# Rotary embedding on one core: who asks for the first rows, and what the first load waits for

## The chip, the core and the metric

The kernel runs on one core of one Trainium2 chip. The metric is the device time of one execution in microseconds (us). The profile describes one execution; its span is the part of it that the trace covers.

## The reference

The input x has 8 batches, 2048 positions, 16 heads and 64 values a head, all float32. Each head's vector is cut into two halves of 32, and the halves are rotated by the cosine and sine of the position:

```python
out1 = x1 * cos - x2 * sin
out2 = x1 * sin + x2 * cos
return np.concatenate([out1, out2], axis=-1)
```

`cos` and `sin` have one row of 32 values for each position. 67.1 MB are read and 67.1 MB are written.

## The kernel before

The 2048 positions are laid over 128 partitions, 16 consecutive positions (called rows here, index j) on each; one batch is a tile of 128 x 16384 elements, held as float16. `buf` has five slots for such tiles, and batch b lies in slot b % 5. The DMA casts float32 to float16 on the way in and back on the way out.

`load`, `store` and `queue` (L57) issue these casting transfers from GpSimd (POOL). `queue` ties each to the one before it, so that all of them stand in one queue in the order that the program writes. This text calls it the ring: the rest of batch 0 (rows 2 to 15), the store of batch 0's row 0, loads of batches 1 and 2 and of 3 and 4, the store of batch 0's other rows, and so on to the store of batch 7's rows 0 to 13. An instruction at the head of POOL's stream that waits for another engine holds up all behind it.

`rotate` is three VectorE instructions on a tile: a product of the swapped halves with signed sine into `v` (L87), a product in place with cosine (L91), and the sum (L93).

Three transfers go by the hardware queues instead: sine by SyncE (SP, L50), cosine by ScalarE (ACT, L51), and `head`, the first two rows of batch 0 on each partition, uncast, by ScalarE (L52). `head` uses the space of slot 4. ScalarE casts sine (L101, and negated in L102) and cosine (L103) to float16 and then the two head rows one after the other (L96). Row 0 is rotated and stored ahead of the rest of batch 0. The loads of batches 3 and 4 need slot 4, and so wait until the head has been cast.

At the end the last two rows of batch 7 are cast to float32 by ScalarE (L127) and stored by SP (L128), after the store of batch 7's rows 0 to 8 has landed.

Of the kernel before, what the change touches and what calls it, by code (L numbers as in the profile page):

```python
# [1 line left out]

# [4 lines left out]


@with_exitstack  # L10
def kernel(
    ctx: ExitStack,
    tc: tile.TileContext,
    x: bass.AP,
    cos: bass.AP,
    sin: bass.AP,
    out: bass.AP,
):
    nc = tc.nc
    f16 = mybir.dt.float16  # L20
    f32 = mybir.dt.float32

    B, S, H, D = x.shape
    Dh = D // 2
    P = nc.NUM_PARTITIONS
    J = S // P
    SLOTS = 5
    JA = 2
    JE = 2
    JF = 1  # L30

    pool = ctx.enter_context(tc.tile_pool(name="rope", bufs=1))
    buf = pool.tile([P, SLOTS, J, H, D], f16)
    v = pool.tile([P, J, H, D], f16)
    sin_f = pool.tile([P, J, Dh], f32)
    cos_f = pool.tile([P, J, Dh], f32)
    cos_h = pool.tile([P, J, Dh], f16)
    sin_h = pool.tile([P, J, D], f16)

    def words(slot, rows):  # L40
        flat = buf[:, slot, 0 : 2 * rows].rearrange("p j h d -> p (j h d)")
        return flat.bitcast(f32)

    head = words(SLOTS - 1, JA)
    tail = words(SLOTS - 2, JE)
    rows_in = x.rearrange("b (p j) h d -> p b (j h d)", j=J)
    rows_out = out.rearrange("b (p j) h d -> p b (j h d)", j=J)
    W = H * D

    nc.sync.dma_start(out=sin_f, in_=sin.rearrange("(p j) d -> p j d", j=J))  # L50
    nc.scalar.dma_start(out=cos_f, in_=cos.rearrange("(p j) d -> p j d", j=J))  # L51
    nc.scalar.dma_start(out=head, in_=rows_in[:, 0, 0 : JA * W])  # L52

    ring = []

    def queue(dst, src):
        dma = nc.gpsimd.dma_start(out=dst, in_=src)  # L57
        if ring:
            tc.add_manual_dep(
                dma.ins,  # L60
                ring[-1].ins.name,
                mybir.DependencyInfo(mybir.DependencyClass.NoSync, mybir.DependencyReason.DATA),
                reason="order of the ring",
            )
        ring.append(dma)
        return dma

    def part(b, n, j0, j1):
        s = b % SLOTS
        return buf[:, s : s + n, j0:j1].rearrange("p n j h d -> p n (j h d)")  # L70

    def load(b, n=1, j0=0):
        return queue(part(b, n, j0, J), rows_in[:, b : b + n, j0 * W : J * W])

    def store(b, n=1, j0=0, j1=J):
        return queue(rows_out[:, b : b + n, j0 * W : j1 * W], part(b, n, j0, j1))

    def rotate(b, j0=0, j1=J):
        n = j1 - j0
        js = slice(j0, j1)  # L80
        xt = buf[:, b % SLOTS, js]
        vt = v[:, js]
        shape = [P, n, H, 2, Dh]
        sin_b = sin_h[:, js, :].rearrange("p j (e d) -> p j e d", e=2).unsqueeze(2).to_broadcast(shape)
        cos_b = cos_h[:, js, :].unsqueeze(2).to_broadcast([P, n, 2 * H, Dh])
        xe = xt.rearrange("p j h (e d) -> p j h e d", e=2)
        nc.vector.tensor_mul(  # L87
            out=vt.rearrange("p j h (e d) -> p j h e d", e=2), in0=xe[:, :, :, ::-1, :], in1=sin_b
        )
        xw = xt.rearrange("p j h (e d) -> p j (h e) d", d=Dh)  # L90
        nc.vector.tensor_mul(out=xw, in0=xw, in1=cos_b)  # L91
        xa = xt.rearrange("p j h d -> p (j h d)")
        nc.vector.tensor_add(out=xa, in0=xa, in1=vt.rearrange("p j h d -> p (j h d)"))  # L93

    def narrow_head(j0, j1):
        nc.scalar.copy(  # L96
            out=buf[:, 0, j0:j1].rearrange("p j h d -> p (j h d)"), in_=head[:, j0 * W : j1 * W]
        )

    load(0, j0=JA)  # L100
    nc.scalar.copy(out=sin_h[:, :, Dh:D], in_=sin_f)  # L101
    nc.scalar.mul(out=sin_h[:, :, 0:Dh], in_=sin_f, mul=-1.0)  # L102
    nc.scalar.copy(out=cos_h, in_=cos_f)  # L103
    narrow_head(0, JF)
    narrow_head(JF, JA)
    rotate(0, 0, JF)
    store(0, j1=JF)
    load(1, 2)
    load(3, 2)
    rotate(0, JF, J)  # L110
    store(0, j0=JF)
    rotate(1)
    rotate(2)
    store(1, 2)
    load(5)
    load(6, 2)
    rotate(3)
    rotate(4)
    store(3, 2)
    rotate(5)  # L120
    rotate(6)
    store(5, 2)
    rotate(7)
    gate = store(7, j1=9)
    store(7, j0=9, j1=J - JE)

    nc.scalar.copy(out=tail, in_=buf[:, (B - 1) % SLOTS, J - JE : J].rearrange("p j h d -> p (j h d)"))  # L127
    end = nc.sync.dma_start(out=rows_out[:, B - 1, (J - JE) * W : J * W], in_=tail)  # L128
    tc.add_manual_dep(
        end.ins,  # L130
        gate.ins.name,
        mybir.DependencyInfo(mybir.DependencyClass.Sync, mybir.DependencyReason.DATA),
        reason="the last rows go out behind this part",
    )


# [1 line left out]
_INS = ['x', 'cos', 'sin']  # L138
_OUTS = [((8, 2048, 16, 64), 'float32')]


# [23 lines left out]
```

## Time and profile before

| what | value |
|---|---|
| median of 3 runs | 316.4 us (316.4 to 316.58) |
| profiled execution | 316.32 us |
| its span | 314.6 us |
| VectorE busy | 209.1 us, 66% of the span |
| ScalarE busy, GpSimd busy | 6.8 us, 7.9 us |
| software queue (ring) | 99.09 MB by its count, 98.1% of the 16 engines' span |
| SP's and ScalarE's hardware queues | 1.31 MB each, 1.2% and 1.0% |

The queue counts bytes by its packets' sizes, which for a casting transfer differ between the two ends; memory's own count is 67.63 MB read and 67.11 MB written. Lines such as L57 refer to the kernel before. "ACTq" and "SPq" are the parts of ScalarE and SyncE that issue transfers. A time line's row has the start, the duration, the engine, the line, the operation and, in brackets, how long the engine had been idle and what ended that.

### The profile page before, as it was taken

To read this page: it belongs to the slowest core of one execution; us is meant where nothing else is said; L and a number is where in the kernel's file an instruction comes from. 1 tells how busy PE (TensorE), PEld (TensorE's weight loads), DVE (VectorE), ACT (ScalarE), POOL (GpSimd) and SP (SyncE) were. 2 spreads that over 40 slices of the span, in tenths; PEclk is the share of its full clock that TensorE was granted. 3 is DMA by queue.
4 is the path that set the end of the run, shared out by engine and by line. 5 is a ranking of instruction groups with operands and counts; after the bars stand their busy time and mean duration, and the time that the engine had idled before them with its cause. 6 is when DMAs were issued, how large, how long until landed. Compare 5 with 4: busy or idle time off the path is not lost.

```text
span 314.6 us, 113 instructions
## 1 busy us (share of the span) xinstructions
DVE 209.1 (66%) x27; ACT 6.8 (2%) x7; POOL 7.9 (3%) x16
## 2 busy tenths in 40 slices
DVE  0109991089999999999994399903999999200000
ACT  3200000000000000000000000000000000200000
POOL 1020000000000000000000000000000000100000
DMA  7989999999999899999999999999999999999998
GB/s 230 261 193 249 267 200 200 200 267 200 200 200 325 375 500 400 400 400 533 400 200 221 246 200 200 250 217 333 400 517 417 400 400 525 408 400 400 433 425 342
DMA packets 3072, 101.71 MB, mean 323 GB/s; under 512 B 256, under 2 KB 256, under 8 KB 640
## 3 DMA queue, kind: packets, MB, share of 16 engines
q0 software_dynamic: 2496, 99.09, 98.1%
q1 hardware_dynamic: 288, 1.31, 1.2%
q10 hardware_dynamic: 288, 1.31, 1.0%
HBM read 67.63 MB, written 67.11 MB: 428 GB/s over the span
## 4 chain that ended last, share of the span: by engine, by line
DVE 59%; DMA 19%; another core or an unknown queue 7%; ACT 1%; issue 0%; POOL 0%; ACTq 0%; DVEq 0%
DVE v L87 20%; DVE buf L91 20%; DVE buf L93 20%; DMA buf<-in_x_dram 19%; ACT buf L127 1%; ACT buf L96 0%; POOL out_dram L57 0%; ACTq L51 0%; DVEq L87 0%
## 5 line engine op out<-in xcount | busy, mean ns | idle before, releaser
L87 DVE TENSOR_TENSOR v<-buf,sin_h 128x16384 f16<-128x16384 f16 (+2 forms) x9 | 69.7, 7744 | 59.7 <-DMA buf<-in_x_dram 45.3
L91 DVE TENSOR_TENSOR buf<-buf,cos_h 128x16384 f16<-128x16384 f16 (+2 forms) x9 | 69.7, 7744 | 0.3
L93 DVE TENSOR_TENSOR buf<-buf,v 128x16384 f16<-128x16384 f16 (+2 forms) x9 | 69.7, 7744 | 0.3
L57 POOL DMA_DIRECT2D out_dram<-buf x7 | 4.3, 620 | 219.7 <-DVE buf L93 219.7
L127 ACT CAST buf<-buf 128x2048 f32<-128x2048 f16 x1 | 1.9, 1897 | 254.2 <-DVE buf L93 254.2
L57 POOL DMA_DIRECT2D buf<-in_x_dram x5 | 3.4, 679 | 43.0 <-DMA out_dram<-buf 42.2
L96 ACT CAST buf<-buf 128x1024 f16<-128x1024 f32 x2 | 2.0, 1042 | 7.2 <-DMA buf<-in_x_dram 7.2
L101 ACT ACT_TABLE_LOAD x1 | 1.3, 1283 | 1.7 <-PEq L149 1.7
L101 ACT CAST sin_h<-sin_f 128x512 f16<-128x512 f32 x1 | 0.6, 617 | 1.5 <-DMA sin_f<-in_sin_dram 1.5
L102 ACT ACTIVATE sin_h<-sin_f 128x512 f16<-128x512 f32 x1 | 0.6, 624 | 0.0
L103 ACT CAST cos_h<-cos_f 128x512 f16<-128x512 f32 x1 | 0.6, 601 | 0.0
L149 POOL MEMSET const-float32-0.0<- 128x1 f32 x1 | 0.1, 99 | 0.2 <-issue 0.2
L149 POOL MEMSET const-bfloat16-1.0<- 128x1 bf16 x1 | 0.1, 102 | 0.0
L149 POOL MEMSET const-float32-1.0<- 128x1 f32 x1 | 0.1, 99 | 0.0
L149 POOL MEMSET const-uint8-127<- 128x1 uint8 x1 | 0.1, 99 | 0.0
## 6 DMA issues: line engine op xcount, KB each, us to landing
buf<-in_x_dram POOLq DMA_DIRECT2D x3, 8192.0 KB, 57.1
out_dram<-buf POOLq DMA_DIRECT2D x1, 7680.0 KB, 71.7
out_dram<-buf POOLq DMA_DIRECT2D x1, 4608.0 KB, 35.5
buf<-in_x_dram POOLq DMA_DIRECT2D x1, 4096.0 KB, 57.3
buf<-in_x_dram POOLq DMA_DIRECT2D x1, 3584.0 KB, 22.6
out_dram<-buf POOLq DMA_DIRECT2D x1, 2560.0 KB, 41.0
buf<-in_x_dram ACTq DMA_DIRECT2D x1, 1024.0 KB, 12.1
out_dram<-buf SPq DMA_DIRECT2D x1, 1024.0 KB, 8.4
```

What stands on the lines that cost most here:

```text
L57: dma = nc.gpsimd.dma_start(out=dst, in_=src)
L87: nc.vector.tensor_mul(out=vt.rearrange("p j h (e d) -> p j h e d", e=2), in0=xe[:, :, :, ::-1, :], in1=sin_b)
L91: nc.vector.tensor_mul(out=xw, in0=xw, in1=cos_b)
L93: nc.vector.tensor_add(out=xa, in0=xa, in1=vt.rearrange("p j h d -> p (j h d)"))
L96: nc.scalar.copy(out=buf[:, 0, j0:j1].rearrange("p j h d -> p (j h d)"), in_=head[:, j0 * W : j1 * W])
L101: nc.scalar.copy(out=sin_h[:, :, Dh:D], in_=sin_f)
L102: nc.scalar.mul(out=sin_h[:, :, 0:Dh], in_=sin_f, mul=-1.0)
L103: nc.scalar.copy(out=cos_h, in_=cos_f)
L127: nc.scalar.copy(out=tail, in_=buf[:, (B - 1) % SLOTS, J - JE : J].rearrange("p j h d -> p (j h d)"))
L149: nc = _bacc.Bacc("TRN2", target_bir_lowering=False, num_devices=1)
```

## The change

SyncE now asks for sine and then for the head. A new tile `word` of two float32 values on each partition is made; VectorE writes a zero into the first, and ScalarE copies it to the second. Two waits on this copy are added: that of ScalarE's request for cosine, and that of the first software load (the rest of batch 0). Nothing else in the program is changed. ScalarE's first instruction that needs an activation table is now this copy, and the table load stands ahead of it.

```diff
     nc.sync.dma_start(out=sin_f, in_=sin.rearrange("(p j) d -> p j d", j=J))
-    nc.scalar.dma_start(out=cos_f, in_=cos.rearrange("(p j) d -> p j d", j=J))
-    nc.scalar.dma_start(out=head, in_=rows_in[:, 0, 0 : JA * W])
+    nc.sync.dma_start(out=head, in_=rows_in[:, 0, 0 : JA * W])
+    word = pool.tile([P, 2], f32)
+    nc.vector.memset(word[:, 0:1], 0.0)
+    warm = nc.scalar.copy(out=word[:, 1:2], in_=word[:, 0:1])
+    cosine = nc.scalar.dma_start(out=cos_f, in_=cos.rearrange("(p j) d -> p j d", j=J))
+    tc.add_manual_dep(
+        cosine.ins,
+        warm.ins.name,
+        mybir.DependencyInfo(mybir.DependencyClass.Sync, mybir.DependencyReason.DATA),
+        reason="the first rows are asked for ahead of cosine",
+    )
...
-    load(0, j0=JA)
+    tc.add_manual_dep(
+        load(0, j0=JA).ins,
+        warm.ins.name,
+        mybir.DependencyInfo(mybir.DependencyClass.Sync, mybir.DependencyReason.DATA),
+        reason="cosine goes ahead of the ring",
+    )
```

## The prediction

> **What bounds the kernel now.** I read the page first, then the waits, then the time line of the first 30 us, then windows over the whole span, and last the trace's records of single DMA packets (start and duration of each), which no printed view lists; where I use those I say so. The page and the waits of the trace:
>
> ```profile
> DVE 209.1 (66%) x27; ACT 6.8 (2%) x7; POOL 7.9 (3%) x16
> q0 software_dynamic: 2496, 99.09, 98.1%
> HBM read 67.63 MB, written 67.11 MB: 428 GB/s over the span
> ...
> POOL out_dram L57 <- DVE buf L93: 219.7, 6, 74.0
> DVE v L87 <- DMA buf<-in_x_dram: 45.3, 4, 15.3
> POOL buf L57 <- DMA out_dram<-buf: 42.2, 2, 38.2
> ```
>
> VectorE is busy two thirds of the span and waits 45.3 us for loads; the software queue that POOL fills is busy 98.1% of it. So the bound is the software queue, called the ring below. The chain that ended last shows 59% VectorE, which misleads: VectorE's next tile is already waiting in the ring while it works. The windows show it:
>
> ```profile
> 30.00:120.00 90.00, 74.41 (x10) 0.00 (x0) 1.26 (x2) 1.00 1.01 265
> 120.00:300.00 180.00, 126.54 (x15) 1.90 (x1) 3.82 (x6) 1.00 1.01 362
> ```
>
> The last-but-one column, the DMA share, is 1.01 in both: the engines move data all the time. The packet records agree: from 2.6 us (second sine packet) to 313.4 us (end of the last row's packets) each engine has a packet in hand. The 134.74 MB read and written, over those 310.8 us, are 433.5 GB/s, and one load packet alone (57,344 bytes read, next one 2.111 us later, on 16 engines) is 434.6 GB/s. No gap is left in the middle to be won. What can change is the stretch before about 6 us:
>
> ```profile
> 0.73 0.39 ACTq L51 DMA_DIRECT2D cos_f<-in_cos_dram  x1
> 0.74 0.38 SPq L50 DMA_DIRECT2D sin_f<-in_sin_dram  x1
> 1.15 0.47 ACTq L52 DMA_DIRECT2D buf<-in_x_dram  x1
> 1.25 0.67 POOL L57 DMA_DIRECT2D buf<-in_x_dram  x1 [0.80 <-PEq L160]
> 1.65 1.28 ACT L101 ACT_TABLE_LOAD   x1 [1.65 <-PEq L149]
> 4.45 0.62 ACT L101 CAST sin_h<-sin_f 128x512 f16<-128x512 f32 x1 [1.52 <-DMA sin_f<-in_sin_dram]
> 5.51 0.60 ACT L103 CAST cos_h<-cos_f 128x512 f16<-128x512 f32 x1
> 13.26 1.99 ACT L96 CAST buf<-buf 128x1024 f16<-128x1024 f32 x2 [7.15 <-DMA buf<-in_x_dram]
> 16.79 0.53 POOL L57 DMA_DIRECT2D out_dram<-buf  x1 [14.88 <-DVE buf L93]
> 17.31 1.43 POOL L57 DMA_DIRECT2D buf<-in_x_dram  x2
> 23.94 8.16 DVE L87 TENSOR_TENSOR v<-buf,sin_h 128x15360 f16<-128x15360 f16 x1 [7.46 <-DMA buf<-in_x_dram]
> ```
>
> Columns: start, duration, engine, line and operation. The packet records put these requests on the engines so: sine from 1.83, cosine mixed in from 2.69, head packets (0.306 us apart, eight on each engine) from 3.95, first ring packet at 5.78 behind six head packets, then ring and head by turns until the head lands at 13.24. The first ring packet is on the engines 4.5 us after POOL began the request at 1.25.
>
> **The change, part by part.**
>
> Head on SP's queue. It leaves ScalarE's queue (a 0.47 us request) for SP's, behind sine's (0.74 to 1.12), so it is asked for at about 1.15 as before. SP has nothing else until its wait for the last rows at 305.26. Cost 0; what hides it is that cosine's 256 KB no longer stand ahead of it.
>
> Memset of the word on VectorE. POOL's 128x1 memsets take 0.10; the shortest VectorE row, 128x1024, takes 0.69; so 0.10 to 0.69, and VectorE starts at about 0.7. I take 0.10, the same shape. Either way it is over by 1.4, under ScalarE's table load. VectorE's next work is at 14.34 before, about 7.9 after.
>
> The table load moves from L101 to the new copy, from 1.65 to about 0.73 (where ScalarE's first request stands), and ends at 2.01. The copy: 128x1024 takes 1.042 and 128x512 0.617, so 0.83 ns an element and 0.19 us that no element explains; one element takes about 0.19 (at most the 0.60 of the shortest row). It ends at about 2.22.
>
> Cosine's request waits for it: 2.25 at the earliest (0.03 between instructions of one engine), 2.5 if the wait costs what POOL's waits for VectorE cost (L93 ends at 16.48, POOL starts at 16.79). Behind it on ScalarE stand the sine and cosine casts and both head casts. Cosine's packets came 1.95 after its request, so now at 4.2 to 4.5; landing came 3.9 after, so about 6.3 instead of 4.6. VectorE waits for that and then for the casts.
>
> The first load waits too, and everything that POOL issues stands behind it. Copy's end 2.22 plus 0.30 is 2.52 instead of 1.25: 1.27 later. This is the one cost that can reach the end, since the ring never pauses afterwards.
>
> What is won at the front: the head, no longer mixed with 57 KB packets, lands near 6.4 instead of 13.24. Casts of cosine (0.60), of the first head row (1.05), three VectorE products (3 x 0.72) and 0.30 put POOL's store near 10.5 instead of 16.79, and the next loads near 11. None of that shortens the ring: its first load still holds the engines until about 23.4, and the trace has the store's packets at 23.36 directly behind it, although they were asked for at 16.79. The store was early by 6.6 us and will be by 13; that is worth 0. Were that cover gone, each us late would cost one.
>
> So the sum is the ring's delay less the short work that fills it. Short work (sine, head, cosine) is the same as before: it would have ended at 5.78 plus two head packets, 6.40. It stays gapless if head packets follow sine's at about 3.2 (their request ends at 1.62; cosine's packets came 1.95 after theirs began, hence 3.1) and cosine comes before the head is done, near 5.7 (4.2 to 4.5: yes). Against it stands the ring: when were its first packets ready before (R)? At the earliest at 1.92, the end of the request. At the latest about 5.0: a cold first packet of sine takes 0.80 against 0.08 later, and the ring's first packet at 5.78 shows no such bubble, so it was in work 0.8 before. The nearest row on how far ahead an engine takes its packets is at the end: SP asks for the last rows at 305.26, packets of such a request appear 1.1 to 1.95 later, but these come at 310.63, behind five ring packets of 0.755 that were taken before them. If six head packets were likewise taken ahead, R is 5.78 less 6 x 0.306 = 3.94. With 1.27 added and 0.78 for the cold first packet, ring data begins at 3.94 + 2.05 = 5.99, before 6.40: no idle time. With R at 5.0 it is 7.05: 0.65 idle. Below nothing I exclude, since the engines cannot begin before sine's first packet at 1.83, which does not move. I take 0.2, nearer the lower end, by the row at the end of the kernel.
>
> A rule bears on R. The Trainium skill (DMA: Bandwidth & Descriptors, Latency and other measured facts) gives a software request about 1 us to its first byte; as an estimate from that page R would be 2.3 before and 3.5 after, the idle time 0 and the time unchanged. The trace shows 4.5 us to the first packet behind a busy queue, which neither confirms nor refutes it.
>
> Sum: the profiled execution took 316.32 (span 314.6 and 1.7 outside it); with 0.2 it is 316.5. The median of the runs is 316.4, 0.08 above the profiled one, so 316.6.
>
> **The rivals.**
>
> (a) Forecast: the short work covers the ring's delay, 0 to 0.6 idle, 316.4 to 317.0. For it: the ring packets that the last rows waited behind. Chance 0.60.
>
> (b) Slower: ScalarE is not ready for the copy when the table load ends. In the trace the next ScalarE instruction came 1.52 us after that load (2.93 to 4.45), put down to sine; that it could have come sooner is not shown. If ScalarE needs most of that time, the copy ends at about 3.7 and POOL's first load begins at 4.0, 2.77 late: ring data from 3.94 + 2.77 + 0.78 = 7.49 to 8.55, and the engines idle 1.1 to 2.15: 317.5 to 318.6. It decides once the first load is 2.31 late with R at 3.94 (3.94 + 2.31 + 0.78 is 6.40 plus 0.63 idle), so with the copy's end at 3.26; with R at 5.0 it decides at once. Against it: the sine's landing at 0.74 + 3.7 = 4.44 explains the wait fully. Chance 0.20. The Trainium skill has a rule of this kind (ScalarE: Activation LUTs, What ACT_TABLE_LOAD costs): 1283 ns for the load, with which the 1.28 here agrees, and about 1380 ns of drain, which no row here shows.
>
> (c) Slower by less: no such pause, but R was late (5.0) and POOL's wait longer than 0.30: idle 0.65 to 1.0, 317.05 to 317.4. Chance 0.13.
>
> (d) Faster: the earlier store and loads close a hole in the ring near 18 to 24 us. The window from 18 to 24 has a DMA share of 0.86 against 0.97 from 300 to 306; read as idle time that is 0.11 x 6 = 0.66 us, 315.7. Against it: the packet records have no gap there, and the low share comes from how long packets that cross a window's edge are counted. Chance 0.07.
>
> (e) That the change does not do what it says is excluded by the order of the built program: ScalarE's stream is table load, copy, cosine; POOL's first load waits for ScalarE; SP's has sine, head.
>
> **How the numbers follow.** A difference of 0.2% (0.63 us) is about what a measurement of this kernel can tell from no change. (a) is same (0.60); (b) and (c) slower (0.33); (d) faster (0.07). The point is that of (a), 316.6. The range begins at 316.1 (0.3 under the median, for run to run and for a different stagger of the 16 engines, 0.25 us apart at the start), takes in (c) and the lower half of (b), and ends at 318.0, which leaves out (d) and half of (b): under 2 in 10.
>
> **What would show it.** Right: the copy ends near 2.2, POOL's first load begins near 2.5, the head lands near 6.4, POOL's store is asked for near 10.5, and yet VectorE's L87 of the first tile's rest (23.94 before) begins at 24.0 to 24.5, with all later work late by the same. Wrong: first load at 3.5 or later and L87 near 25 or beyond (b); or L87 before 23.9 and SP's last request before 305.2 (d). If L87 is not late but the end is, the cause lies behind the first load and my accounting of one gapless stream falls.

## The result, and the profile after

The changed kernel takes 321.58 us (median of 6 runs, 318.31 to 322.22) against 316.46 us before (316.3 to 316.61). The ratio is 1.0149, with a 95% interval of 1.0123 to 1.0174: slower by 5.1 us, where 316.6 was forecast and 318.0 was the end of the range. One of the six runs took 318.31 and was not profiled; the other five took 321.5 to 322.2. The profiled execution took 321.77 us, its span 320.0 us, 5.4 more than before.

The time line of the changed kernel (start, duration, engine, line, operation; L54 and L55 are the copy and cosine's request, L66 is the ring, L96 VectorE's first product), and from the page the landing times of three requests:

```profile
0.74 1.28 ACT L54 ACT_TABLE_LOAD   x1 [0.74 <-PEq L163]
2.04 0.19 ACT L54 COPY word<-word 128x1 f32<-128x1 f32 x1
2.26 0.36 ACTq L55 DMA_DIRECT2D cos_f<-in_cos_dram  x1
2.53 0.67 POOL L66 DMA_DIRECT2D buf<-in_x_dram  x1 [2.08 <-ACT word L54]
21.72 0.62 ACT L117 CAST cos_h<-cos_f 128x512 f16<-128x512 f32 x1 [17.24 <-DMA cos_f<-in_cos_dram]
22.25 1.99 ACT L105 CAST buf<-buf 128x1024 f16<-128x1024 f32 x2
25.77 0.53 POOL L66 DMA_DIRECT2D out_dram<-buf  x1 [22.57 <-DVE buf L102]
26.30 1.43 POOL L66 DMA_DIRECT2D buf<-in_x_dram  x2
68.17 8.69 DVE L96 TENSOR_TENSOR v<-buf,sin_h 128x16384 f16<-128x16384 f16 x1 [18.25 <-DMA buf<-in_x_dram]
```

```profile
buf<-in_x_dram SPq DMA_DIRECT2D x1, 1024.0 KB, 4.8
...
cos_f<-in_cos_dram ACTq DMA_DIRECT2D x1, 256.0 KB, 19.4
```

Copy, cosine's request and first load stand where the prediction put them (2.03, 2.25, 2.52), and the head lands 4.8 after its request, at about 6. But cosine lands 19.4 us after its request instead of 3.9. ScalarE takes its work in order, so both head casts wait for cosine's cast, and with them the rotation of row 0 and POOL's store, at 25.77 instead of 16.79. Behind that store stand the next loads.

The windows of the changed kernel around that time (last two columns: DMA share, GB/s), and its ring on the page:

```profile
18.00:23.00 5.00, 0.00 (x0) 1.28 (x2) 0.00 (x0) 1.00 0.86 184
23.00:27.00 4.00, 3.61 (x4) 1.23 (x2) 1.23 (x2) 1.00 0.04 14
27.00:31.00 4.00, 4.00 (x1) 0.00 (x0) 0.73 (x2) 1.00 1.11 256
...
q0 software_dynamic: 2496, 99.09, 97.0%
HBM read 67.63 MB, written 67.11 MB: 421 GB/s over the span
```

From 23 to 27 us the engines move next to nothing: the first load is done and the ring is empty. The kernel before has no such window:

```profile
20.00:25.00 5.00, 1.06 (x1) 0.00 (x0) 0.00 (x0) 1.00 1.23 301
25.00:30.00 5.00, 5.00 (x1) 0.00 (x0) 0.00 (x0) 1.00 0.97 210
```

A window can count a packet whole that reaches into the next (from 19 to 20 us the kernel before has a share of 2.13, from 20 to 21 one of 0.00), so the hole is measured from packets. A second loss is not seen in such windows. The completion records of the ring's transfers (mean over the 16 engines, us) show both:

```
                       before    after    difference
first load              23.40    23.25    -0.15
store of row 0          24.63    28.22    +3.59
load of batches 1, 2    63.28    67.62    +4.34
load of batches 3, 4   101.90   107.32    +5.41
store of batch 0's rest 119.99   125.41    +5.41
last part of the ring  310.72   316.13    +5.41
```

The hole is 3.75 us (28.22 less 23.25, less the store's own 1.22). Behind it the two loads take 39.40 and 39.70 us instead of 38.65 and 38.63, together 1.8 more. After 107 us nothing is added. Packet and completion times in this text, as in the prediction, count from a zero about 0.07 us earlier than that of the time lines.

The packet records show how cosine got there. Its packets begin on all engines at 5.25 to 5.46, directly behind the head; the ring's first packets come at 5.72 to 6.42. On 11 engines all eight cosine packets were through by then (completions by 6.41). On five they were not, and from there one 2 KB packet of cosine went for each 57 KB packet of the ring, about 2.2 us a turn: completions at 14.92, 15.03, 19.08, 19.57 and 21.41. A transfer has landed when its last engine has.

**Theory 1**: that mixing, the late store behind it and the hole make the loss. **Theory 2** (rival): the ring's later start makes it. The 1.8 us of slow loads got theories of their own later.

### The profile page after: what moved, and what is told of

Its sections match the earlier page's. It is cut to its first block, busy times and chain, and to the rows that moved or that the text cites. A ratio compares the mean times of both kernels' runs of the same rounds, so it can differ in the third digit from the quotient of the medians.

```text
span 320.0 us, 115 instructions
## 1 busy us (share of the span) xinstructions
DVE 209.1 (65%) x28; ACT 7.0 (2%) x8; POOL 7.9 (2%) x16
## 4 chain that ended last, share of the span: by engine, by line
DVE 58%; DMA 19%; another core or an unknown queue 7%; ACT 2%; issue 0%; POOL 0%; DVEq 0%
DVE v L96 19%; DVE buf L100 19%; DVE buf L102 19%; DMA buf<-in_x_dram 13%; DMA cos_f<-in_cos_dram 6%; ACT buf L141 1%; ACT L54 0%; ACT buf L105 0%; ACT cos_h L117 0%; POOL out_dram L66 0%; ACT word L54 0%; DVEq L96 0%
## 5 line engine op out<-in xcount | busy, mean ns | idle before, releaser
L96 DVE TENSOR_TENSOR v<-buf,sin_h 128x16384 f16<-128x16384 f16 (+2 forms) x9 | 69.7, 7744 | 64.4 <-DMA buf<-in_x_dram 41.8
L66 POOL DMA_DIRECT2D out_dram<-buf x7 | 4.3, 620 | 223.2 <-DVE buf L102 223.2
L66 POOL DMA_DIRECT2D buf<-in_x_dram x5 | 3.4, 679 | 44.9 <-DMA out_dram<-buf 42.8
L54 ACT COPY word<-word 128x1 f32<-128x1 f32 x1 | 0.2, 192 | 0.0
```

Source lines behind the costliest of these rows:

```text
L54: warm = nc.scalar.copy(out=word[:, 1:2], in_=word[:, 0:1])
L96: nc.vector.tensor_mul(out=vt.rearrange("p j h (e d) -> p j h e d", e=2), in0=xe[:, :, :, ::-1, :], in1=sin_b)
```

## The experiments

Each ratio is to the kernel before, measured beside it, with its 95% interval.

**Cosine asked for at once, the load still waiting.**

```diff
+    nc.scalar.dma_start(out=cos_f, in_=...)     # ahead of sine's request, no wait
     nc.sync.dma_start(out=sin_f, in_=...)
     nc.sync.dma_start(out=head, in_=...)
...
-    cosine = nc.scalar.dma_start(out=cos_f, in_=...)
-    tc.add_manual_dep(cosine.ins, warm.ins.name, ...)
```

> The changed kernel, but cosine is asked for by ScalarE at once, ahead of the table load and of the copy; the first software load still waits for the copy (it will start near 2.9, as the request now stands ahead of the copy). Theory 1 (cosine's late request lets its packets take turns with the ring's 2.1 us packets on some engines; it lands at 21.7, the head casts stand behind it on ScalarE, POOL's store of row 0 comes at 25.8 and the ring runs dry from 23.1 to 27.0): cosine lands near 5, the store is asked for before 12, no hole, 316.4 to 317.0. Theory 2 (what costs is the ring's own later start, 2.53 instead of 1.25): the load is as late or later, so 321 or more.

Measured: 316.47 us, ratio 1.0002 (0.9994 to 1.0011). Its time line:

```profile
2.95 0.67 POOL L60 DMA_DIRECT2D buf<-in_x_dram  x1 [2.51 <-ACT word L55]
5.29 0.60 ACT L111 CAST cos_h<-cos_f 128x512 f16<-128x512 f32 x1
10.49 0.53 POOL L60 DMA_DIRECT2D out_dram<-buf  x1 [6.87 <-DVE buf L96]
```

The first load begins 1.7 later than before (1.25), later still than in the changed kernel, and that costs nothing. Cosine's wait is the part that costs. Theory 2 falls.

**The load free, cosine still waiting.** Only the wait of `load(0, j0=JA)` is taken out of the changed kernel.

> The changed kernel, but the first software load does not wait (starts at 1.25 as in the kernel before); cosine still waits for the copy. Theory 1: the ring is there before cosine, cosine takes turns with it on all 16 engines (eight packets of each engine, 2.2 us a turn, from about 5), lands between 20 and 24, the store comes between 24 and 28, hole of 2 to 5 us, 319 to 323. Theory 2 (the ring's late start costs): 316.4.

Measured: 323.98 us, 1.0239 (1.0226 to 1.0252), worse than the whole change and a little beyond what was expected. All 16 engines now mix: cosine's completions lie between 22.9 and 23.9. The time line, and the window in which the ring is empty:

```profile
24.37 0.62 ACT L112 CAST cos_h<-cos_f 128x512 f16<-128x512 f32 x1 [19.68 <-DMA cos_f<-in_cos_dram]
28.43 0.53 POOL L66 DMA_DIRECT2D out_dram<-buf  x1 [26.52 <-DVE buf L102]
...
23.00:27.00 4.00, 1.00 (x2) 2.51 (x3) 0.00 (x0) 1.00 0.02 5
```

The hole is 6.45 us, and the wait on the load, which the prediction counted as the only cost, is what kept 11 engines of the changed kernel clear of the ring.

**The load still later.** In the changed kernel the first load waits for a second ScalarE copy, behind cosine's request.

```diff
+    nc.vector.memset(v[:, 0, 0:8, :], 0.0)
+    later = nc.scalar.copy(out=v[:, 1, 0:8, :], in_=v[:, 0, 0:8, :])   # ordered behind cosine's request
     tc.add_manual_dep(
         load(0, j0=JA).ins,
-        warm.ins.name,
+        later.ins.name,
```

> The changed kernel with the first software load waiting longer: for a second ScalarE copy (512 float32-free elements into an unused part of v, about 0.6 us) that stands behind cosine's request, so the load starts near 3.6 instead of 2.53. Theory 1: all of cosine is through (near 6.4) before the ring's first packet (near 6.8); cosine lands near 6.5, no hole; the engines idle about 0.4; 316.6 to 317.2. Theory 2: slower than the changed kernel, by about 1 or more: 322 to 324.

Measured: 316.77 us, 1.0018 (1.001 to 1.0027); single runs from 316.65 to 317.87.

```profile
3.58 0.67 POOL L66 DMA_DIRECT2D buf<-in_x_dram  x1 [3.13 <-ACT v L110]
6.60 0.62 ACT L125 CAST cos_h<-cos_f 128x512 f16<-128x512 f32 x1 [1.93 <-DMA cos_f<-in_cos_dram]
10.65 0.53 POOL L66 DMA_DIRECT2D out_dram<-buf  x1 [6.41 <-DVE buf L102]
```

One us more of waiting wins 4.8 us back: cosine lands at 6.6 and the hole is gone. What is left, 0.39 us, fits the price of a late ring that the prediction had put at 0 to 0.65. The ring's first packets came at 6.00 to 6.34 here, the earliest about 2.4 after the request.

**The next load ahead of the store.** Cosine stays late; two neighbours of the ring are exchanged.

```diff
-    store(0, j1=JF)
     load(1, 2)
+    store(0, j1=JF)
     load(3, 2)
```

> The changed kernel with two neighbours of the ring exchanged: the load of batches 1 and 2 goes ahead of the store of batch 0's row 0. Cosine, the head casts and the first rotation stay as late as they are (21.7, 22.3, 23.3). Theory 1, its second half (the time is lost because POOL's store of row 0 stands ahead of the next load and the ring runs dry): no hole at 23 to 27, load of batches 1 and 2 lands at 62 to 63, 316.3 to 317.0. Rival (VectorE's first rotation at 23.3 instead of 14.3 costs by itself, or the engines run slower after a mixed start): 318 or more.

Measured: 317.34 us, 1.0031 (1.0021 to 1.0041); single runs from 316.43 to 318.53.

```profile
22.43 0.62 ACT L117 CAST cos_h<-cos_f 128x512 f16<-128x512 f32 x1 [17.70 <-DMA cos_f<-in_cos_dram]
26.46 0.57 POOL L66 DMA_DIRECT2D out_dram<-buf  x1 [22.55 <-DVE buf L102]
...
23.00:27.00 4.00, 2.91 (x4) 1.94 (x3) 0.54 (x1) 1.00 1.03 221
```

Cosine, casts and store are as late as in the changed kernel, and the window that was empty is full: most of the loss needs the hole. About 1 us stays, more than expected. The last round of packets (one packet on each engine) of the exchanged load took 2.92 us instead of 2.43, although this load was asked for at about 3.2 and stands behind no hole. In the profiled execution (318.53) one engine had mixed to the end (22.17); it finished the first load 1.1 behind the mean and the store of row 0 1.9 behind, and from there the 16 engines' completions were 2.34 apart to the end (before: 0.29). The latest engine's last completion is 2.2 later than before, as is the span (316.8 against 314.6). In the changed kernel the engines were 0.8 apart at the first load's end and 0.15 behind the hole, where all wait for the same request; without a hole one engine's delay is carried to the end.

**The late store by itself.** In the kernel before, `pad(n)` copies n rows of sine into an unused part of `v` on ScalarE, ahead of the head casts; requests and waits stay.

```diff
+    last = pad(15)
+    last = pad(3)
-    narrow_head(0, JF)
+    n0 = narrow_head(0, JF)      # ordered behind `last`
```

> The kernel before (requests and waits as they are), with two long ScalarE copies of sine into an unused part of v (15 and 3 rows, about 13.0 and 2.8 us) ahead of the head casts, so that the casts begin near 21.9 as in the changed kernel and POOL's store of row 0 comes near 25.4; cosine is not mixed with the ring. Theory 1: the ring runs dry from 23.6 to about 26.6, and the loss is that of the changed kernel less the 0.4 by which the store is sooner: if the loads behind the hole run slow because of the hole itself (or of VectorE's work beside it), 320.5 to 321.5; if they run slow because cosine put the engines out of step, only the hole is lost, 319 to 320. Rival (the cause is not the hole): 316.4.

Measured: 321.06 us, 1.0149 (1.0136 to 1.0162).

```profile
5.33 0.60 ACT L104 CAST cos_h<-cos_f 128x512 f16<-128x512 f32 x1
25.04 0.53 POOL L57 DMA_DIRECT2D out_dram<-buf  x1 [23.12 <-DVE buf L93]
...
23.00:27.00 4.00, 3.93 (x4) 0.49 (x1) 1.96 (x3) 1.00 0.28 96
```

The store is asked for at 25.04, the hole is 2.93 us, and the loads behind it take 39.54 and 39.49. With cosine cast at 5.33 and not mixed with the ring the loss is there: the slow loads belong to the hole or to the late requests, not to cosine.

**The store later, but in time.** `pad(13)` alone.

> As the run before, with one ScalarE copy of 13 rows (11.3 us): the casts begin near 17.4, POOL's store comes near 20.9, 4.1 later than in the kernel before but 2.5 before the ring has worked off its first load (23.4). Theory 1: no hole, 316.3 to 316.7. Rival (each us of the store's lateness costs): about 318 to 320.

Measured: 318.3 us, 1.0047 (1.0028 to 1.0066); four runs at 318.3 to 318.6 and two at 316.7 and 316.8. The expectation holds for 316.7 alone, with 316.8 close by; the other four, and the median, lie in the rival's range. The profiled execution is the one at 316.83: store at 20.62, no hole, the second load 38.96 instead of 38.63. The four at 318.3 to 318.6 were not profiled; their 1.9 to 2.2 is close to the price of the slow loads, but no trace shows where it went. That a store which is late but in time costs nothing is therefore not shown.

**A hole with VectorE idle.** As the late store, with VectorE's rest of the first tile held until a further ScalarE copy of 6 rows is done.

> The kernel with the late store (copies of 15 and 3 rows), and VectorE's work on the rest of the first tile held back by one more ScalarE copy (6 rows, to about 29.5), so that VectorE does nothing while POOL asks for the store and the two loads behind the hole (25.4 to 27.5). If the slow loads behind the hole (39.4 and 39.7 us in the changed kernel against 38.65 and 38.6) come from VectorE working while their descriptors are written, they are back at 38.6 here and the time is 1 to 1.7 under that of the late store alone; if not, the two are equal within 0.3.

Measured: 320.99 us, 1.0144 (1.0131 to 1.0157), loads 39.54 and 39.42. VectorE began at 28.54, after POOL's three requests (24.84 to 26.79), and nothing changed. The Trainium skill (SBUF — State Buffer, Who interferes with whom) says that some VectorE instructions can hold up the writing of software descriptors, and that `tensor_tensor`, the kind used here, was not seen to do so; with 320.99 against 321.06 this run agrees, and VectorE is not what slows these loads.

**The head on SyncE alone.** In the kernel before, `nc.scalar` becomes `nc.sync` in the head's request.

> One part of the change alone: the head is asked for by SyncE behind sine; cosine stays with ScalarE at 0.73, no word, no copy, no waits. Both theories: nothing waits, the head is through at about 6 to 13 and POOL's store is asked for before 17; 316.2 to 316.6. If it is 318 or more, the head's place in SyncE's queue is at fault, not cosine.

Measured: 316.42 us, 1.0003 (0.9994 to 1.0011). This part of the change is free, as forecast.

**Four engines out of step, and the control.** One SyncE request more in the kernel before, for 4 or for 16 partitions.

```diff
+    nc.sync.dma_start(out=v[0:4, 2:6]..., in_=rows_in[0:4, 0, 0 : 2 * W])     # control: 0:16
```

> Open so far: behind the hole both loads run slow (39.5 us each instead of 38.65, the first and the last round of packets most) although neither cosine's mixing nor VectorE is needed for that, and some executions without a hole lose 1 to 2 us too. This run is the kernel before with one more SyncE request behind sine: 4 partitions by 8 KB of x into an unused part of v, which go to 4 of the 16 engines, one packet of 0.31 us each; so 4 engines are 0.31 out of their usual step, with no hole and cosine early. Theory 3 (the engines' places against each other, set at the start and at a hole, decide whether the loads run clean): the loads show rounds above 2.432 us and a long last round; more than 0.31 is lost, 317.0 to 318.5, or the time varies between executions. Rival (only a hole or a late request makes loads slow): 316.4 to 316.75, all loads at 38.65.

> Control for the run with 4 partitions: the same request for 16 partitions by 8 KB, one packet on each of the 16 engines, so that all are 0.31 late and their places against each other stay. Both theories: 316.7 (0.31 more than before), loads at 38.65, little spread.

Measured: 317.25 us, 1.003 (1.0019 to 1.004), and 317.5 us, 1.0054 (1.0032 to 1.0075; single runs 317.31 to 319.94). The first lies in theory 3's range, but its trace refutes the theory: the engines are 1.11 us apart to the end and every load round stays at 2.432. The loss is the latest engine's delay (first load's last completion 24.61 against 23.60; span 315.6 against 314.6). The control's expectation failed: one more packet on each engine cost 1.07 at the first load's end instead of 0.31, which was not followed up, and two of its seven runs took 319.14 and 319.94 without a profile.

**A small hole.** The late store with `pad(1)` instead of `pad(3)`.

> The kernel with the late store, but copies of 15 and 1 rows instead of 15 and 3: the casts begin near 19.8 and POOL's store comes near 23.4, its packets near 24.6 (1.2 after the request, as behind the hole of the changed kernel), so the hole is about 1.2 instead of 2.9 (run with 15 and 3 rows: 26.2 against 23.4). If the slow loads cost a fixed amount behind any hole: 316.4 + 1.2 + 1.7 = 319.3. If their cost grows with the hole: about 318.3. If the hole alone costs: 317.6.

Measured: 319.18 us, 1.0089 (1.0075 to 1.0104). Store at 23.40, hole 1.25, loads 39.57 and 39.38. Holes of 1.25, 2.93 and 3.75 us have slow loads worth 1.67, 1.75 and 1.82, and the hole of 6.45 (load free) has 1.65: nearly a fixed price, which does not grow with the hole.

**Cosine behind the head in SyncE's queue.**

```diff
     nc.sync.dma_start(out=head, in_=...)
+    nc.sync.dma_start(out=cos_f, in_=...)
-    cosine = nc.scalar.dma_start(out=cos_f, in_=...)
-    tc.add_manual_dep(cosine.ins, warm.ins.name, ...)
```

> The changed kernel with cosine asked for by SyncE, behind the head in the same queue (request near 1.6 instead of 2.26, no wait for the copy); the first software load still waits for the copy (2.53). Theory 1, in the form that what counts is when cosine's packets come on the engines against the ring's first packet: behind the head they cannot come before about 5.2, where they also came in the changed kernel, with the ring at 5.7 to 6.4, so some engines mix again: 318 to 322, varying. Rival (the time of the request counts; 0.6 sooner is enough): 316.4 to 316.7.

Measured: 316.61 us, 1.0012 (1.0004 to 1.0021); single runs 316.4 to 317.96. My expectation was wrong, the rival's right for most runs.

```profile
1.63 0.42 SPq L52 DMA_DIRECT2D cos_f<-in_cos_dram  x1
2.52 0.67 POOL L60 DMA_DIRECT2D buf<-in_x_dram  x1 [2.08 <-ACT word L55]
10.33 0.53 POOL L60 DMA_DIRECT2D out_dram<-buf  x1 [7.14 <-DVE buf L96]
```

With the load at the same 2.52, asking for cosine 0.63 sooner and in the head's queue is enough; which of the two did it was not separated. Cosine's packets were not sooner on the engines: the first begins at 5.42 here and at 5.25 in the changed kernel. It is the ring's first packet that came later, from 6.06 instead of 5.72, and none stood between cosine's packets. In the profiled execution, one of the longer ones at 317.4, the engines were 1.17 apart to the end.

**A longer first store behind the hole, and its control.** `JF = 2`, so that rows 0 and 1 are cast, rotated and stored as one; with `pad(15)`, and without.

> The kernel with the late store (one ScalarE copy of 15 rows ahead of the head casts), but with the first store twice as long: rows 0 and 1 are cast, rotated and stored as one (JF = 2), so that the casts begin near 18.9, POOL's store comes near 24.9 as in the first late-store run (25.0), and its packets hold the engines about 2.4 us instead of 1.2, in which the descriptors of the next load can become ready. Theory 4 (the 1.7 us that every hole so far cost beyond its length is paid because the load behind the short store starts cold: not ready when the store ends, its first round 0.5 longer, nothing read ahead): the first round of the load is back at 2.43 to 2.5 and about 1 us or more is won back, 319.0 to 320.0. Rival (fixed price of any hole): 320.8 to 321.3 as in the first late-store run.

> Control for the longer first store: the kernel before with JF = 2 and no copy that delays anything. The store is asked for near 19.0 instead of 16.8, well before 23.4: 316.3 to 316.7, by both theories.

Measured: 320.41 us, 1.0123 (1.0108 to 1.0139), and 317.05 us, 1.0024 (1.0016 to 1.0033). Mean duration of the first and last rounds of packets of the two loads (us):

```
                       batches 1, 2     batches 3, 4
                       first   last     first   last
before                 2.431   2.432    2.431   2.432
changed kernel         2.893   2.443    2.431   3.326
late store             2.876   2.450    2.431   3.190
late, longer store     2.674   2.432    2.431   3.324
two rows, no delay     2.469   2.432    2.431   2.776
```

Theory 4 is half right. With time to get ready under a longer store, the first load took 38.99 instead of 39.54, and 0.65 us came back, less than the 1 or more expected; the hole was also shorter, 2.66 instead of 2.93. The last round of the second load stayed at 3.3. Its cause is open: it comes with holes, smaller with requests in time but late (the control asked at 21.3 instead of 19.0), and also at the end of the exchanged load, which was asked for early. The control was expected at 316.3 to 316.7 and missed.

## Why the prediction was wrong

- **The step that failed: cosine's landing.** "Cosine's packets came 1.95 after its request, so now at 4.2 to 4.5; landing came 3.9 after, so about 6.3". The packets came at 5.25, behind the head's, and the landing took 19.4. Both terms were carried over from a row in which cosine had only sine beside it. The same section used the row that says otherwise: the head, 1 MB, landed 12.1 us after its request because its last two packets took turns with the ring. I applied that to the head and not to the transfer that now stood in its place. My own sum had the warning: it begins the ring's data at 5.99, has cosine land near 6.3 and ends the short work at 6.40. I read that as "no idle time"; it also means that the last packets of the short work stand beside the ring's and take turns with them, as cosine's did on five engines.
- **The cover that was "worth 0" was gone.** The prediction said that the store's earliness hides nothing and that, were it gone, "each us late would cost one". With the store at 25.77 the ring was dry for 3.75. The condition was named, but no rival was worked out for it.
- **R, the time at which the ring is ready.** I put it 2.7 after POOL's request by a row of the kernel's end, and the sum that used it was near: 5.99 for the ring's data, 5.72 to 6.42 measured. R itself stays open. Behind the hole, with idle engines, the first packet came 1.1 after the request (25.77 to 26.88 on the time line's zero). The Trainium skill (DMA: Bandwidth & Descriptors, Latency and other measured facts) has about 1 us, with which this agrees. By the 1.1 alone the ring would have been ready near 3.6 in the changed kernel and there before cosine's first packet at 5.25; on all 16 engines it came behind it.
- **A hole's price.** "Each us late would cost one" was too low: 1.65 to 1.82 us came on top of the holes ahead of the short store (1.25 to 6.45 us long), and about 1.2 on top of the one ahead of the longer store.
- **What held.** The copy ran from 2.04 to 2.23 and the load began at 2.53; a later ring alone cost 0 to 0.4 (316.47 with the load at 2.95, 316.77 at 3.58); the head on SyncE is free; no hole lay near 18 to 24 in the kernel before (rival d). Rival (b) fell: ScalarE ran the copy 0.02 after the table load, so no pause follows it here. Slower had a chance of 0.33, for other reasons.

In sum the profiled execution's 5.4 are -0.15 at the start, 3.75 of hole and 1.82 in the two loads. Nothing tried here beats the kernel before: its engines have work from 2.6 to 313.4 us.

## What to carry to other kernels

Where a small transfer and a saturated queue of large packets share the engines, the small one lands with its last packet's turn: ask for it early enough that all of it is through first (316.47 here), or hold the queue back until it is nearly through. The wait has to be set by when packets reach the engines and not by the request: a load at 2.53 was too soon (321.58), one at 3.58 late enough (316.77). A wait for the landing itself, at 6.6, was not tried. Before moving a request, list what is queued behind its landing on the engine that consumes it, in that engine's order. A queue kept full by a chain of waits has one reserve, the time between a request and the moment that its predecessor is worked off; find that number and ask what would eat it. Using up part of it was not free here either: the runs with the store at 20.6 and 21.3 lost 1.9 and 0.6 us on the median, with no hole in their profiles.

## What was not expected of the hardware

- Cosine's 256 KB took 19.4 us beside the ring and 3.9 beside sine, by one packet for one packet: 2 KB against 57 KB.
- A hole of 1.25 us cost 2.8, one of 3.75 about 5.4, one of 6.45 cost 7.6: the loads behind a hole lose 1.65 to 1.82, most of it in the first round of the first and the last round of the second. Why the last round is long stays open.
- One engine's delay at the start is kept: engines 0.29 us apart (before), 1.1 or 2.3 apart (runs with four engines late, with the exchanged load) stay so for 250 to 290 us, and the time follows the latest.
